# Who issues the stores: gate chunks and the high halves of queries and keys go from ScalarE's queue to SyncE's, and the load of `b_f` goes to the front

## The chip, the cores and the metric

One Trainium2 chip, of which one core is used. The metric is the time of one execution on the device, in microseconds (us). TensorE (PE) multiplies, VectorE (DVE), ScalarE (ACT) and GpSimd (POOL) work on elements, and SyncE (SP) does nothing but issue transfers. Each engine has a queue of its own and works through it in order. A transfer (DMA) is issued by an instruction in one of these queues; the data then move by themselves, and a counter (semaphore) tells when they have landed.

## The reference

One step of a hybrid encoder layer, for a prompt of 1024 rows and a sample of 64 (1088 rows together), in float32. Cut to what matters:

```python
xn = rms_norm(x, g_pre)
xa, ga, q, k, v, gb, fl, ma, mb = split(xn @ w_in)       # widths 7 x 1024 + 16 + ...
logf = log_sigmoid(fl + b_f)
ya = rg_lru(causal_conv(xa)) * silu(ga)                  # branch A, a recurrence over the rows
yb = attention(q, k, v, bias=cumsum(logf)) * silu(gb)    # branch B, 16 heads of 64, causal
u = (ya @ w_branch[0], yb @ w_branch[1])
mix = (sigmoid(ma) * u[0] + sigmoid(mb) * u[1]) @ w_o
h = x + rms_norm(mix, g_post)
y = h + rms_norm(sigmoid(h @ w_ple_gate) * (pe @ w_ple_proj), g_ple)
```

The keys, values, `logf` and the last states are outputs too. The sample attends to a cache of 128 rows as well.

## The kernel before

Every float32 factor is split into a high and a low part, and a product takes three passes on TensorE (high by high, low by high, high by low). ScalarE makes the high part (`copy_act`, L82), VectorE subtracts it from the whole to get the low part (`sub`, L85). So each panel of weights goes through ScalarE and VectorE before TensorE can use it: `w_raw` becomes `wh` and `wl`, and in the opening `wv_raw` becomes `wvh` and `wvl` (the fourth and fifth slices of the value weights are loaded into `w_raw`).

The stages, in order of time:

- **Opening** (to about 125 us). The rows are normalised and turned, and the values (`vacc`, `v_sb`) and the forget logits `fl` are made block by block. `load_wv` (L348) and `load_x` (L338) load on SyncE; `b_f`, which is added to `fl`, is loaded by ScalarE at L505. In the opening the order of ScalarE and VectorE is written out by hand, and each of their instructions stands in the queue where the code says.
- **Plain panels** (to about 162 us). Gate panels: `panel_steps` multiplies a panel of 128 columns by all rows in three chunks, and `spill` (L304) takes each finished chunk out of PSUM into an `st` tile (two buffers) with ScalarE and stores it to memory, to be read again at the end (`d_ma`, `d_mb`, `d_gb` hold the gates of branch A, branch B and the attention's own gate).
- **Quad stage** (about 162 to 430 us). Queries, keys and some gate columns are made by a scheme of seven products for eight (`quad`, L805). `put` (L829) takes a finished half out, and for queries and keys makes a high half `oh` (two buffers) with ScalarE and a low half `kl` or `ko` with VectorE. Both are stored, to be read again by the heads.
- **Attention** (about 437 to 861 us). Sixteen heads, two at a time. Heads load their queries and keys a head ahead. `load_v` (L1069) reads the values of a pair in two halves into `v_raw`, which has one buffer; GpSimd splits them into `vv` (L1077, L85). Scores, softmax (the normalisation is GpSimd's `tensor_scalar`, L1110), transposes (`tp`, split by ScalarE into `th` and by VectorE into `tl`), the product with `vv` (`pv`, L1175 and L1177), and the output `y` (VectorE, L1186) to `d_y` (SyncE, L1162). In between TensorE's time is filled with the chunks of further gate panels, whose `st` is stored by `spill`.
- **Branch A, projections, merge, norms** (from 861 us on). The gates are read back, the recurrence runs, and the last products are made.

TensorE's order is written out by hand from beginning to end. In the attention a planner puts the work of ScalarE, VectorE and GpSimd at booked times (`book`), and the instructions then stand in that order. SyncE's order is the compiler's, except that the four loads of a weight panel keep their order in the program (`load_panel`, L254).

Of the transfers that the change touches, ScalarE issues the stores of `spill`, that of the high half in `put`, and four of the quad stage's gate columns (L838, where the half has no second summand). All other loads and stores are on SyncE already, but for `g8` (L441), the stores of the values (L528) and a few of GpSimd's.

Of the kernel before, what the change touches and what calls it, by code (L numbers as in the profile page):

```python
# [13 lines left out]
P = 128  # L14
# [17 lines left out]
HT = T // 2  # L32
# [33 lines left out]
def hybrid_step(tc, a, o):  # L66
    nc = tc.nc
    PSUM = bass.MemoryType.PSUM
    act, dve, pool, pe, sp = nc.scalar, nc.vector, nc.gpsimd, nc.tensor, nc.sync
# [8 lines left out]
    def f(ap):  # L78
        return ap.bitcast(F32)

    def copy_act(out, in_, scale=1.0):
        return act.activation(out=out, in_=in_, func=AF.Copy, scale=scale)  # L82
# [221 lines left out]
    def spill(dst, t0, n, z, s=None):  # L304
        s = s or wpool.tile([P, GC], F32, name="st")
        copy_act(s[:, :n], z)
        act.dma_start(dst[:, t0:t0 + n], s[:, :n])


    mm = ps("mm", bufs=2)  # L310
# [11 lines left out]
    bf = p1.tile([P, NH], F32, name="bf")  # L322
# [12 lines left out]
    def load_x(b):  # L335
        src, n, _ = x_src[b]
        t = p1x.tile([P, D], F32, name="x_in", tag="x_in", bufs=2)
        sp.dma_start(t[:n, :], src)  # L338
        x_in.append(t)
# [3 lines left out]
    def load_wv(k):  # L343
        if k in (3, 4):
            raw = raw_half[k - 3]
        else:
            raw = p1x.tile([P, D], F32, name="wv_raw", tag="wv_raw", bufs=3)
        sp.dma_start(raw[:, :], w_in[k * P:(k + 1) * P, C_V:C_V + D])  # L348
        raws[k] = raw
# [89 lines left out]
    gT = p1.tile([P, KT], F32, name="gT")  # L439
    load_x(0)  # L440
    act.dma_start(g8[:, :], a["g_pre"].rearrange("(k p) -> k p", p=P))  # L441
    load_wv(0)
    load_x(1)
    for k in range(1, KT):
# [57 lines left out]
    sp.dma_start(g_pre[:, :], a["g_pre"].partition_broadcast(P))  # L502
    load_x(2)
    load_x(3)
    act.dma_start(bf[:, :], a["b_f"].partition_broadcast(P))  # L505
    sp.dma_start(lp[:, :], a["cache_logf"])

    vec = p1.tile([96, P], F32, name="vec")
# [1 line left out]
    for name in ("conv_w", "conv_b", "b_rg_a", "b_rg_x", "a_param", "state_h", "state_conv"):  # L510
        n = a[name].shape[0]
# [70 lines left out]
    for b in range(2, NBLK + 1):  # L582
        _, n, t0 = x_src[b]
# [47 lines left out]
    def gate_panel(tag, w, room=lambda c: None):  # L631
        return panel_steps(mm, *w, xs, lambda c, t0, n, z: spill(tag[1], t0, n, z, room(c)))
# [176 lines left out]
    def keys_out(p, ss, c0, t0, blocks):  # L809

        cols = slice(p * P, (p + 2) * P)
        tp = mm.tile([P, 512], F32, name="tpk", tag="acc")
        c = c0
        for i, n in enumerate(blocks):
            for j, s in enumerate(ss):
                pe.transpose(tp[:n, (2 * i + j) * P:(2 * i + j + 1) * P], s[:, c:c + n], ident[:, :])
            c += n
        for i, n in enumerate(blocks):
            n_st[0] += 1
            st = (wpool.tile([P, GC], F32, name="st") if n_st[0] % 3 else  # L820
                  sp_.tile([P, 2 * P], F32, name="kst", tag="kst", bufs=1))
            copy_act(st[:n, :2 * P], tp[:n, 2 * i * P:2 * (i + 1) * P])
            dst = o["k_prompt"][t0:t0 + n, cols] if t0 < SEQ else o["k_sample"][:, cols]
            sp.dma_start(dst, st[:n, :2 * P])
            t0 += n
# [3 lines left out]
    def put(kind, arg, z, in1, h):  # L829

        s = kqp.tile([P, HT], F32, name="ko", tag="ko", bufs=4)
        s3 = s.rearrange("p (c n) -> p c n", c=2)
        if in1 is None:
            copy_act(s3, z)
        else:
            dve.tensor_tensor(out=s3, in0=z, in1=in1, op=ALU.add)
        if kind == "r":
            (act if in1 is None else sp).dma_start(arg[:, h * HT:(h + 1) * HT], s[:, :])  # L838
            return
        d = d_k if kind == "k" else d_q  # L840
        h_ = slice(h * HT, (h + 1) * HT)
        hi = sp_.tile([P, HT], F32R, name="oh", tag="oh", bufs=2)
        scale = 1.0 if kind == "k" else HD ** -0.5
        copy_act(hi[:, :], s[:, :], scale)
        act.dma_start(d[0, arg][:, h_], f(hi[:, :]))
        lo = sp_.tile([P, HT], F32, name="kl", tag="kl", bufs=1) if kind == "k" else s
        dve.scalar_tensor_tensor(out=lo[:, :], in0=s[:, :], scalar=scale, in1=f(hi[:, :]),
                                 op0=ALU.mult, op1=ALU.subtract)
        sp.dma_start(d[1, arg][:, h_], lo[:, :])
        if kind == "k":  # L850
            kept[arg, h] = s
            p = arg - arg % 2
            if (p, h) in kept and (p + 1, h) in kept:
                ss = [kept.pop((p + j, h)) for j in range(2)]
                c = 0
                for blocks in ((P, P), (P, P), (HT - 4 * P,)) if h == 0 else ((P, P), (P, SEQ - HT - 3 * P), (DEC,)):
                    owed.append((n_prod[0] + 1, lambda c=c, blocks=blocks: keys_out(p, ss, c, h * HT + c, blocks)))
                    c += sum(blocks)

    def seven(i, w, ahead_, last):  # L860
# [28 lines left out]
        if last:  # L889
            mul(tcc, w["s1"], T1, True)  # L890
            for j, t in enumerate(blk(0, 1)):
                sp.dma_start(f(t), d_b12[j])
        mul(ta, w["a12"], B21, False)
        put(*d1, za, None, 0)
        more()
        mul(tb, w["s3"], T3, False)
# [3 lines left out]
        if not last:  # L900
            mul(tcc, w["s1"], T1, True)
        put(*d2, zc, u3, 1)
        mul(tb, w["a22"], T4, False)
        put(*d2, zb, p1, 0)
        more()
        mul(tcc, w["s4"], B22, False)
# [131 lines left out]
    def filler():  # L1038
        left = deque()
        nxt = first_fill  # L1040
        while True:
            if nxt is None:
                look_ahead()
                if not ahead or ahead[0][0][0] != "r":
                    return
                nxt = ahead.popleft()[:3:2]
            (_, dst), w = nxt
            nxt = None
            book_split()

            def evac(c, t0, n, z, dst=dst):
                def do():
                    spill(dst, t0, n, z)
                    left.popleft()

                left.append(book("A", now[0] + 497.0 + HOP_PE, A_ST, do))

            for _ in panel_steps(mm, *w, xs, evac):
                spent(497.0)
                if len(left) > 1:  # L1060
                    catch_up(left[0])
                yield True
# [552 lines left out]
    tag, w = panel()  # L1615
    assert tag == ("f", KT - 1)
    fill = panel_steps(mm, *w, xs, lambda c, t0, n, z: spill(d_mb[KT - 1], t0, n, z))
    chunk(fill)
    early_gate(k - 1)
# [530 lines left out]
    n = x_src[b][1]  # L2150
# [68 lines left out]
```

## Time and profile before

| | us |
|---|---|
| median of three runs | 1465.84 |
| the three runs | 1465.83, 1465.84, 1467.97 |
| the profiled execution | 1464.86 |
| its span in the trace | 1463.1 |
| TensorE busy | 1435.9 |
| VectorE busy | 890.9 |
| ScalarE busy | 717.6 |
| GpSimd busy | 301.8 |

The span goes from the first to the last instruction of the trace; 1.8 us of the execution lie around it. Busy time does not count the instructions that issue transfers. A queue's name with a q (ACTq, SPq) stands for the sequencer that issues: in a row with ACTq, ScalarE is held by an issue. The clock of TensorE has two levels, 1.2 and 2.4 GHz; PEclk gives the granted clock as a share of the higher one.

### The profile page before, as it was taken

To read this page: it belongs to the slowest core of one execution; us is meant where nothing else is said; L and a number is where in the kernel's file an instruction comes from. 1 tells how busy PE (TensorE), PEld (TensorE's weight loads), DVE (VectorE), ACT (ScalarE), POOL (GpSimd) and SP (SyncE) were. 2 spreads that over 40 slices of the span, in tenths; PEclk is the share of its full clock that TensorE was granted. 3 is DMA by queue.
4 is the path that set the end of the run, shared out by engine and by line. 5 is a ranking of instruction groups with operands and counts; after the bars stand their busy time and mean duration, and the time that the engine had idled before them with its cause. 6 is when DMAs were issued, how large, how long until landed. Compare 5 with 4: busy or idle time off the path is not lost.

```text
span 1463.1 us, 25647 instructions
## 1 busy us (share of the span) xinstructions
PE 1435.9 (98%) x9653; PEld 1394.3 (95%) x9653; DVE 890.9 (61%) x1631; ACT 717.6 (49%) x1353; POOL 301.8 (21%) x385
## 2 busy tenths in 40 slices
PE   8999999999999999999899999999999999999997
PEld 8999999999999999999899989999999999879997
DVE  5464866564325666666466555988735474778534
ACT  4423444442215566656466556777534332554633
POOL 0013324323113333333233220221014100000001
PEclk9999999999999999999999999999999999999999
DMA  8457456754276675646554444454269674224111
GB/s 288 141 119 109 139 153 188 182 174 127 81 213 157 119 147 136 142 116 137 109 134 121 76 97 76 90 84 94 75 226 314 242 240 155 97 91 159 51 42 44
DMA packets 149304, 200.64 MB, mean 137 GB/s; under 512 B 24212, under 2 KB 115836, under 8 KB 148156
## 3 DMA queue, kind: packets, MB, share of 16 engines
q1 hardware_dynamic: 129772, 167.06, 44.1%
q10 hardware_dynamic: 17680, 25.64, 5.1%
q0 software_dynamic: 1728, 6.29, 2.3%
q8 instruction: 76, 1.25, 0.4%
q14 instruction: 48, 0.39, 0.1%
HBM read 131.04 MB, written 65.80 MB: 135 GB/s over the span
## 4 chain that ended last, share of the span: by engine, by line
PE 78%; DVE 7%; DMA 6%; ACT 4%; issue 2%; POOL 1%; SPq 1%; ACTq 0%; DVEq 0%; POOLq 0%
PE quad L805 16%; PE acc L170 10%; PE acc L172 10%; PE acc L171 10%; PE tp L1147 4%; PE q L1866 4%; PE pv L1175 3%; PE s L1125 2%; PE pv L1177 2%; PE s L1126 2%; DMA gb_in<-d_gb 2%; PE vacc L170 1%; PE vacc L171 1%; PE vacc L172 1%; POOL yb_in L1671 1%
## 5 line engine op out<-in xcount | busy, mean ns | idle before, releaser
L170 PE MATMUL acc<-xh,wh 128*128 128x364 f32 (+1 forms) x768 | 253.3, 330 | 0.3 <-ACT st L82 0.2
L171 PE MATMUL acc<-xl,wh 128*128 128x364 f32 (+1 forms) x768 | 252.1, 328 | 0.0
L172 PE MATMUL acc<-xh,wl 128*128 128x364 f32 (+1 forms) x768 | 252.0, 328 | 0.0
L170 PEld LDWEIGHTS acc<-xh,wh 128*128 128x128 f32 x768 | 145.0, 189 | 1.7 <-ACT st L82 0.9
L171 PEld LDWEIGHTS acc<-xl,wh 128*128 128x128 f32 x768 | 144.8, 189 | 0.6
L172 PEld LDWEIGHTS acc<-xh,wl 128*128 128x128 f32 x768 | 144.5, 188 | 0.0
L1105 DVE CUSTOM_DVE_ANT_0 s<-s,mask 128x1024 f32<-128x1024 f32 (+7 forms) x128 | 95.5, 767 | 27.7 <-PE s L1126 27.4
L85 DVE TENSOR_TENSOR wl<-w_raw,wh 128x1024 fp32r<-128x1024 f32 (+1 forms) x53 | 60.0, 1134 | 72.1 <-ACT wh L82 71.3
L1110 POOL TENSOR_SCALAR pb<-pb,sm 128x896 f32<-128x896 f32 (+1 forms) x64 | 61.9, 967 | 196.3 <-DVE sm L1109 175.9
L82 ACT ACTIVATE wh<-w_raw 128x1024 fp32r<-128x1024 f32 (+1 forms) x65 | 63.2, 974 | 67.8 <-PE quad L805 26.0
L85 DVE TENSOR_TENSOR tl<-tp,th 128x512 fp32r<-128x512 f32 x96 | 65.8, 688 | 35.8 <-ACT th L82 35.8
L805 PE MATMUL quad<-xh,wh 128*128 128x272 f32 x384 | 80.7, 291 | 0.0
L805 PE MATMUL quad<-xl,wh 128*128 128x272 f32 x384 | 79.5, 288 | 0.0
L805 PE MATMUL quad<-xh,wl 128*128 128x272 f32 x384 | 79.4, 288 | 0.0
L82 ACT ACTIVATE th<-tp 128x512 fp32r<-128x512 f32 x96 | 57.0, 597 | 40.8 <-PE tp L1147 33.3
L1107 ACT ACTIVATE pb<-s,nm 128x896 f32<-128x896 f32 (+1 forms) x64 | 61.1, 955 | 30.1 <-DVE nm L1105 27.7
L1125 PE MATMUL s<-k,q 128*128 128x256 f32 (+1 forms) x192 | 67.4, 354 | 0.2 <-ACT pb L1107 0.2
L1147 PE MATMUL tp<-ident,pb 128*128 128x128 f32 x416 | 64.1, 275 | 1.2 <-DVE diag0l L85 0.7
L1126 PE MATMUL s<-k,q 68*128 68x256 f32 (+1 forms) x192 | 65.2, 351 | 0.0
L171 PE MATMUL acc<-ybl,wh 128*128 128x364 f32 (+1 forms) x192 | 63.0, 328 | 0.9 <-DVE ybl L85 0.9
L170 PE MATMUL acc<-ybh,wh 128*128 128x364 f32 (+1 forms) x192 | 62.8, 327 | 0.2 <-ACT ybh L82 0.2
L172 PE MATMUL acc<-ybh,wl 128*128 128x364 f32 (+1 forms) x192 | 62.8, 327 | 0.0
(713 smaller groups left out, 4154.2 us busy)
## 6 DMA issues: line engine op xcount, KB each, us to landing
w_raw<-in_w_in SPq DMA_DIRECT2D x56, 256.0 KB
q<-d_q SPq DMA_DIRECT2D x48, 256.0 KB
k<-d_k SPq DMA_DIRECT2D x48, 256.0 KB
w_raw<-in_w_in SPq DMA_DIRECT2D x64, 128.0 KB
w_raw<-in_w_branch SPq DMA_DIRECT2D x32, 256.0 KB
wl<-w_raw POOLq DMA_DIRECT2D x12, 512.0 KB, 4.6
wraw<-in_w_in SPq DMA_DIRECT2D x20, 256.0 KB
d_k<-oh ACTq DMA_DIRECT2D x16, 272.0 KB
```

The source lines that it names most:

```text
L82: return act.activation(out=out, in_=in_, func=AF.Copy, scale=scale)
L85: return eng.tensor_tensor(out=out, in0=in0, in1=in1, op=ALU.subtract)
L170: pe.matmul(out, ah, bh, start=start, stop=False)
L171: pe.matmul(out, ah, bl, start=False, stop=False)
L172: pe.matmul(out, al, bh, start=False, stop=stop)
L805: pe.matmul(acc[:, c, :CW], l[:, k, :], r[:, k, c * CW:(c + 1) * CW], start=(first and k == 0 and p == 0), stop=(k == 3 and p == 2), skip_ ...
L1105: at = book("D", now[0] + HOP_PE, per(D_MAX, n), lambda: dve.tensor_tensor_reduce(out=s[:, :n], in0=s[:, :n], in1=m, scale=-1.0, scalar=-N ...
L1107: free = book("A", at, per(A_EXP, n), lambda: act.activation(out=pr[:, :n], in_=s[:, :n], func=AF.Exp, scale=-1.0, bias=nm, accum_out=sm))
L1110: return free, book("G", at, per(G_NORM, n), lambda: pool.tensor_scalar(out=pr[:, :n], in0=pr[:, :n], scalar1=sm, scalar2=1.0, op0=ALU.mul ...
L1125: pe.matmul(s[:, c0:c0 + w], t["q1"][:, q0:q0 + P], t["k1"][:, c0:c0 + w], start=True, stop=False)
L1126: pe.matmul(s[:, c0:c0 + w], t["q2"][:HD + 4, q0:q0 + P], t["k2"][:HD + 4, c0:c0 + w], start=False, stop=True)
L1147: pe.transpose(tp[:, o0 + i * P:o0 + (i + 1) * P], pr[par][:, kb * P:(kb + 1) * P], ident[:, :])
```

## The change

Stores in `spill` and in `put` are issued by SyncE in place of ScalarE, and the load of `b_f` is issued by ScalarE right behind that of `g8`, in place of behind the fourth load of `x`. ScalarE keeps these two loads and the stores of the values.

```diff
     def spill(dst, t0, n, z, s=None):
         s = s or wpool.tile([P, GC], F32, name="st")
         copy_act(s[:, :n], z)
-        act.dma_start(dst[:, t0:t0 + n], s[:, :n])
+        sp.dma_start(dst[:, t0:t0 + n], s[:, :n])
...
     act.dma_start(g8[:, :], a["g_pre"].rearrange("(k p) -> k p", p=P))
+    act.dma_start(bf[:, :], a["b_f"].partition_broadcast(P))
     load_wv(0)
     load_x(1)
...
     load_x(2)
     load_x(3)
-    act.dma_start(bf[:, :], a["b_f"].partition_broadcast(P))
     sp.dma_start(lp[:, :], a["cache_logf"])
...
         if kind == "r":
-            (act if in1 is None else sp).dma_start(arg[:, h * HT:(h + 1) * HT], s[:, :])
+            sp.dma_start(arg[:, h * HT:(h + 1) * HT], s[:, :])
             return
...
         copy_act(hi[:, :], s[:, :], scale)
-        act.dma_start(d[0, arg][:, h_], f(hi[:, :]))
+        sp.dma_start(d[0, arg][:, h_], f(hi[:, :]))
```

## Rows read from the trace of the kernel before

**Rows 1.** The page's first part: busy time of each engine, its share, its instructions.

```profile
PE 1435.9 (98%) x9653; PEld 1394.3 (95%) x9653; DVE 890.9 (61%) x1631; ACT 717.6 (49%) x1353; POOL 301.8 (21%) x385
```

**Rows 2.** TensorE's waits: line, what it waited for, total us, times, longest.

```profile
PE pv L1175 <- DVE y L1186: 4.6, 2, 4.0
PE vacc L471 <- ACT wvh L82: 3.0, 2, 1.9
...
PE quad L805 <- DVE u__1643 L887: 0.9, 1, 0.9
```

**Rows 3.** The table by stretches: length, busy times, PEclk, DMA share, GB/s.

```profile
23.93:31.64 7.71, 7.48 (x37) 7.06 (x38) 6.96 (x13) 5.29 (x8) 0.00 (x0) 0.78 0.95 336
...
714.63:720.72 6.09, 6.09 (x22) 5.91 (x23) 3.73 (x9) 3.37 (x7) 1.38 (x2) 0.50 0.10 24
```

**Rows 4.** Timeline of ScalarE, 18 to 34: start, length, line, idle time before.

```profile
18.85 0.90 ACT L82 ACTIVATE xh<-tp,gT 128x128 fp32r<-128x128 f32 x3
...
22.82 2.00 ACT L82 ACTIVATE wvh<-w_raw 128x1024 fp32r<-128x1024 f32 x2 [3.07 <-DMA vec<-in_conv_b]
...
27.96 1.06 ACT L82 ACTIVATE wvh<-wv_raw 128x1024 fp32r<-128x1024 f32 x1 [1.04 <-DMA wv_raw<-in_w_in]
```

**Rows 5.** The chain of waits, 13 to 45: start, length, what held it.

```profile
14.31 8.06 DMA vec<-in_conv_b
...
22.40 0.38 ACTq L505
...
31.80 5.72 PE vacc L471 x36
```

**Rows 6.** Timeline of ScalarE, 708 to 714.

```profile
708.65 0.46 ACT L82 ACTIVATE st<-acc 128x360 f32<-128x360 f32 x1
...
712.93 0.60 ACT L82 ACTIVATE th<-tp 128x512 fp32r<-128x512 f32 x1 [3.81 <-DMA v_raw<-out_v_prompt]
```

**Rows 7.** The chain of waits, 690 to 716.

```profile
692.15 7.87 DMA d_mb<-st
...
700.50 6.61 DMA v_raw<-out_v_prompt
...
709.56 2.90 DMA v_raw<-out_v_prompt
...
712.53 0.35 ACTq L307
...
714.16 0.42 DVE y L1186
```

**Rows 8.** Timeline of TensorE, 14 to 37.

```profile
21.67 0.32 PE L471 MATMUL acc<-wvl,xh 128*128 128x346 f32 x1
23.93 0.58 PE L471 MATMUL vacc<-wvh,xh 128*128 128x346 f32 x2 [1.94 <-ACT wvh L82]
...
35.93 0.64 PE L471 MATMUL vacc<-wvh,xh 128*128 128x346 f32 x3
```

**Rows 9.** Issues by line: durations in ns (min/median/max), first and last start.

```profile
L307 ACTq DMA_DIRECT2D d_mb<-st x24: 326/326/393, 559.0 to 1029.9; - x24
...
L845 ACTq DMA_DIRECT2D d_k<-oh x16: 326/326/358, 165.4 to 312.1; - x16
```

**Rows 10.** Timeline of TensorE, 709 to 711.

```profile
710.02 0.60 PE L1147 MATMUL tp<-ident,pb 128*128 128x128 f32 x4
```

**Rows 11.** The chain of waits, 128 to 165.

```profile
132.33 0.34 ACTq L307
```

**Rows 12.** Timelines of SyncE and of ScalarE, 748 to 763.

```profile
750.09 6.48 SPq L254 DMA_DIRECT2D w_raw<-in_w_in  x4
...
751.04 0.33 ACTq L307 DMA_DIRECT2D d_gb<-st  x1
```

**Rows 13.** Timelines of GpSimd, 704 to 716 and 758 to 769.

```profile
707.17 0.40 POOL L1077 CAST vv<-v_raw 128x256 fp32r<-128x256 f32 x1 [4.84 <-DMA v_raw<-out_v_prompt]
...
767.88 0.42 POOL L1110 TENSOR_SCALAR prs<-prs,sm 128x192 f32<-128x192 f32 x1 [3.27 <-DVE sm L1109]
```

## The prediction

> **What bounds the kernel now.** I read the page's busy shares first. TensorE is busy for 1435.9 us of the 1463.1 us span [rows 1], so a change of who issues a store can win only where TensorE stands still or runs slowly, some 27 us in all. The list of TensorE's waits comes next: the longest single stops are one of 4.0 us in front of `pv` and one of 1.9 us in front of `vacc` [rows 2]. The table by stretches shows what follows such a stop: from 23.93 to 31.64 the granted clock is 0.78 on average, and from 714.63 to 720.72 it is 0.50, the 1.2 GHz level, with TensorE busy throughout [rows 3]. A stop is thus paid for twice. TensorE's other idle time is in pieces under 1.1 us, the start (1.6 us) and the tail.
>
> Then the chain of waits around both stops, and the timelines of ScalarE and TensorE beside it. Both stops start in ScalarE's queue, at an issue that the change moves.
>
> **First stop: `b_f`.** ScalarE finishes `xh` at 19.75 (18.85 and 0.90) and does nothing until 22.82 [rows 4]. In between its queue holds the issue of `bf`, at 22.40, which the chain puts down to the transfer of `conv_b` that SyncE issued at 14.31 and that needed 8.06 us [rows 5]. `bf` needs nothing of `conv_b`: the two share a completion counter, and the issuing engine waits in order. The split `wvh` stands right behind it. The reader is to see that the idle time in front of `wvh` is put down to that same transfer, not to its own weights: they were there.
>
> **Second stop: `d_mb`.** ScalarE copies `st` at 708.65 for 0.46, so it is free at 709.11, and starts `th` at 712.93 [rows 6]. In between lies the issue of the store of `st`, at 712.53, held by a transfer of `v_raw` that SyncE issued at 709.56 [rows 7]. Up the chain the same pair is tied the other way: a `v_raw` load at 700.50 came late because SyncE had waited for a store of `d_mb` that needed 7.87 us from 692.15.
>
> **The change, part by part.** *The load of `b_f`.* Early in the queue it waits for nothing, and costs ScalarE one issue of 0.38 us [rows 5] before its first work, which waits for `x` in any case; I take nothing for it (at most 0.4 us). The split can then start at 19.75 in place of 22.82. TensorE's last matmul ahead of the stop starts at 21.67, 0.16 after the one before, so the next can start at 21.83 in place of 23.93 [rows 8]. From there to 31.64 it does 36 matmuls; as many at full clock take 5.72 us from 31.80 on [rows 5]. So they would be done at 21.83 + 5.72 = 27.55 in place of 31.64: 4.1 us; with a small new stop, 4.0. If the lower clock stayed, only the stop would go, 1.9 us [rows 2]. What is late next: the last `wv_raw` piece, whose split runs at 27.96 for 1.06 [rows 4]. TensorE takes its slice at 35.93 now [rows 8] and at 31.9 then, so nearly 3 us are left for VectorE's half.
>
> *Stores of gate chunks (L307).* The 24 of `d_mb` take 0.326 us each to issue, the 16 of `d_k` by L845 the same [rows 9]; with 21 of `d_ma`, 12 of `d_gb`, 16 of `d_q` and seven single ones 96 stores leave ScalarE, 31 us of its queue. Nearly all of it is beside the path, as ScalarE has slack. At 709.11, though, it matters: `th` starts then, 3.8 us sooner, and with it `y` at 714.16 - 3.8 = 710.4 for 0.42. TensorE ends its transposes at 710.02 + 0.60 = 710.62 [rows 10], so a stop of about 0.25 is left of 4.00: 3.75 us won. Behind it, 6.09 us were done at half clock [rows 3]; at full clock they take 3.05, as much again. Sum 6.8 us; if the stop stays, nothing.
>
> *Plain panels.* There the chain runs through the issues of L307 themselves, at 132.33 for 0.34 and once more at 152.61 [rows 11], and ends in a stop of 0.9 in front of the first quad product [rows 2]. Taking two issues out gives up to 0.67; the bounds are nothing and 0.9. I take 0.5.
>
> *High halves of query and key, and the four of L838.* They go from ScalarE to SyncE in the quad stage, where the list of waits has one stop over 0.5 us, behind VectorE; I take nothing for them, their cover being TensorE's own matmuls.
>
> **What it adds.** SyncE gets 96 issues more, and it is in order: a store at the head of its queue waits for ScalarE's copy, and each load behind it waits too. One place: SyncE issues four `w_raw` loads from 750.09 on for 6.48 us, while the copy for a store ends at 751.0 and the store leaves ScalarE at 751.04 [rows 12]. Put in front of those loads, it holds them by 0.95 us. What I would fear for is `v_raw`, which has a single buffer and feeds GpSimd. There the trace has one lateness for comparison: GpSimd waited 4.84 us for `v_raw` at 707.17 without a stop of TensorE at that place, and after another pair it stood idle for 3.27 us ahead of 767.88 [rows 13]. Some 3 us of lateness are thus covered by GpSimd's own idle time; behind that its normalisations come late, and TensorE after them. Bounds: nothing, if each delay stays under 3 us, and one stop like that at 714.63 (6.8 us) for each pair of heads that is hit, of which there are seven. As the holds that I can read are nearer 1 us than 3, I take 1 us for small delays.
>
> **The sum.** The profiled execution took 1464.86 us, 0.98 under the median of 1465.84. 1464.86 - 4.0 - 6.8 - 0.5 + 1.0 = 1454.6; beside the median, 1455.5.
>
> **A rule that speaks against it.** The two stops show an issue that cost ScalarE 3.07 and 3.81 us of idle time, ten times its own 0.33. The Trainium skill, "DMA: Bandwidth & Descriptors", section "Issuing engines are not separate DMA queues", says that transfers started by different engines share the same 16 DMA engines, and that spreading the issue saves only the sequencer's time, usually small. By that rule alone the change would be worth the two 0.33 us issues on the chain, and the time about 1465.2. The rows differ from it here, as what ScalarE saves is the wait in front of the issue.
>
> **Rivals.** *One stop comes back.* The wait at 709 is a coincidence of which transfer has the same counter as the store. If SyncE's queue holds `v_raw` or a buffer so that something else is late there, only the start and the panels gain: 1465.84 - 4.0 - 0.5 = 1461.3. For it: the chain there is made of two queues that wait for one another [rows 7], and SyncE is one of them. Against: without the store, nothing in ScalarE's queue waits for SyncE at 709.
>
> *Nothing to be seen.* TensorE stops just as long for another reason behind the same places, or the delays on SyncE give all back: about 1465. By the rule above it is the expected case; the rows above speak against it.
>
> *Slower: the store at the head of SyncE's queue.* SyncE carries the loads of `v_raw`, heads and weights; if its order has stores ahead of them, `v_raw` comes more than 3.3 us late, GpSimd is late with its normalisations, and TensorE stops as it did at 714.63. Against the 11.3 us won, it decides from the third such stop on: 1465.84 - 11.3 + 3 x 6.8 = 1474.9. For it: `v_raw` has one buffer, and SyncE has waited for stores already [rows 7]. Against: 4.84 us of lateness at 707.17 passed without a stop [rows 13].
>
> **How the numbers follow.** A measurement of this kernel tells about 0.2% (2.9 us) from no change. Chances: all three gains, 0.61; one stop back, 0.16; nothing to be seen, 0.13 (with up to two new stops); slower, 0.10. So faster 0.77, same 0.13, slower 0.10. The likeliest is 1455.5, by itself within 1451.5 (0.9 for the panels, no cost on SyncE, some more idle pieces closed) and 1459 (the start at 1.9, or 3 us of delays). The range reaches over the second and third cases, 1451 to 1467, and leaves out the slower one and a little below.
>
> **What the next profile would show.** Right: ScalarE's `wvh` follows `xh` at about 19.8 with no idle time, and the granted clock stays full from there to 40; TensorE's list of waits has no `pv` over 1 us, and the clock is full around 710 as well; the stretch from the quad stage to the tail as long as before. Wrong: a new stop in the head pairs with a half clock behind it, and GpSimd's `vv` waiting for `v_raw` ahead of it; or `w_raw`, queries or keys that come after TensorE wants them. The forecast fails if the order of SyncE's queue is changed so that loads wait for copies by more than 3 us, or if the stops merely move to another store that shares a counter with a late load.

## The result: a little slower, as a new stop takes back what two old ones gave

The changed kernel takes 1468.24 us (median of 22 runs, 1464.60 to 1471.68) where the kernel before takes 1465.84 (22 runs, 1460.98 to 1468.36). The ratio is 1.0024, with an interval of 1.0017 to 1.0032: slower by a quarter of a per cent, and 1.2 us above the range that was forecast. The profiled execution of the changed kernel took 1469.88 us with a span of 1467.9, that is 4.8 us above the span before.

The page of the changed kernel gives TensorE's busy time first (it answers to [rows 1]), and the list of TensorE's waits follows (it answers to [rows 2]; columns as there).

```profile
PE 1433.2 (98%) x9653; PEld 1392.0 (95%) x9653; DVE 894.2 (61%) x1631; ACT 714.6 (49%) x1353; POOL 296.1 (20%) x385
```

```profile
PE acc L170 <- ACT st L82: 12.0, 3, 10.2
...
PE pv L1175 <- DVE y L1186: 1.1, 2, 0.6
PE vacc L472 <- ACT wvh L82: 1.1, 1, 1.1
```

Both old stops are gone: no `pv` waits for more than 0.6 us, where it was 4.0, and the 1.1 us left in front of `vacc` is another stop, ahead of 14 us, which was there before as well. In their place stands one wait of 10.2 us in front of `acc`, for ScalarE's copy `st`. The table by stretches of TensorE (length, busy time, PEclk, DMA share, GB/s; it answers to [rows 3]) shows what this costs.

```profile
22.00:40.00 18.00, 18.00 (x118) 1.00 0.95 307
...
442.09:448.00 5.91, 5.91 (x20) 0.50 1.01 276
707.00:722.00 15.00, 14.35 (x102) 1.00 0.70 111
```

The full clock now holds from 22 to 40 and from 707 to 722. The lower level of 1.2 GHz has moved to the 5.9 us behind the new stop.

The table compares the two traces by the same matmul at each border of a stage: its start in the kernel before is taken from its start in the changed kernel. A minus is time won.

| stretch (by the times before) | us won or lost in it | sum so far |
|---|---|---|
| start to 31.6, the first stop | -4.0 | -4.0 |
| to 161.9, plain panels | +0.5 | -3.5 |
| to 412.5, quad stage | +0.7 | -2.8 |
| to 459.9, start of the attention | +13.0 | +10.2 |
| to 707.9, attention | +0.6 | +10.8 |
| to 720.7, the second stop | -6.7 | +4.1 |
| to the end | +0.6 | +4.8 |

So the two gains came in the size that was forecast, 4.0 and 6.7 us. The loss of 13 us at the start of the attention was not in the sum: 10.2 us are the stop, and 5.9 us at half clock behind it are 2.95 us more than at full clock. The chain of waits of the changed kernel leads to its cause (start, length, what held it).

```profile
424.55 10.76 DMA k<-d_k
435.37 0.27 SPq L1090
...
438.69 0.59 SPq L1097
439.38 2.07 DMA d_ma<-st
441.56 0.48 ACT st L82
```

The timelines of SyncE, ScalarE and TensorE in that stretch show the rest.

```profile
417.22 1.95 SPq L254 DMA_DIRECT2D w_raw<-in_w_in  x4
...
438.20 1.08 SPq L1097 DMA_DIRECT2D qsl<-d_q  x2
439.38 1.00 SPq L307 DMA_DIRECT2D d_ma<-st  x2
...
442.06 0.92 SPq L307 DMA_DIRECT2D d_ma<-st  x2
```

```profile
420.05 0.47 ACT L82 ACTIVATE st<-acc 128x364 f32<-128x364 f32 x1 [6.23 <-PE acc L172]
423.96 0.48 ACT L82 ACTIVATE st<-acc 128x364 f32<-128x364 f32 x1 [3.44 <-PE acc L172]
441.56 1.06 ACT L82 ACTIVATE st<-acc 128x360 f32<-128x360 f32 x2 [17.12 <-DMA d_ma<-st]
```

```profile
442.09 0.67 PE L170 MATMUL acc<-xh,wh 128*128 128x364 f32 x1 [10.16 <-ACT st L82]
```

The first two chunks of the attention stage are copied at 420.05 and 423.96, and both `st` tiles are then full. Their stores leave SyncE only at 439.38, behind 25 loads that begin at 417.22: four of weights, eight for the first head, two of values, eleven for the sample (my expectations below say 26 and twelve). These loads in turn wait for one another in order; the one of `cs_k` at 435.37 was let go by a load of `k` that needed 10.76 us. The instruction records of the traces show why: the transfers of SyncE and ScalarE are dealt out to eight completion counters, SyncE's loads here in turn, so that each stands behind the transfer eight before it; `cs_k` and that load of `k` both have counter 105. In the kernel before, the pairs of the two old stops share a counter in the same way, 109 for `conv_b` and `b_f`, 105 for `v_raw` and the store at 712.53. ScalarE waits 17.12 us for a free `st`, the PSUM banks of `acc` stay full, and TensorE stops for 10.16 us. In the kernel before, ScalarE issued the same two stores at 423.40 and 427.31, between SyncE's loads.

### The profile page after: what moved, and what is told of

Its sections match the earlier page's. It is cut to its first block, busy times and chain, and to the rows that moved or that the text cites. A ratio compares the mean times of both kernels' runs of the same rounds, so it can differ in the third digit from the quotient of the medians.

```text
span 1467.9 us, 25740 instructions
## 1 busy us (share of the span) xinstructions
PE 1433.2 (98%) x9653; PEld 1392.0 (95%) x9653; DVE 894.2 (61%) x1631; ACT 714.6 (49%) x1353; POOL 296.1 (20%) x385
## 4 chain that ended last, share of the span: by engine, by line
PE 79%; DMA 7%; DVE 6%; ACT 4%; issue 2%; SPq 1%; POOL 1%; DVEq 0%; ACTq 0%; POOLq 0%
PE quad L805 16%; PE acc L170 10%; PE acc L171 10%; PE acc L172 10%; PE q L1866 5%; PE tp L1147 4%; PE pv L1175 2%; PE s L1125 2%; PE s L1126 2%; PE pv L1177 2%; DMA gb_in<-d_gb 2%; PE vacc L170 1%; PE vacc L171 1%; PE vacc L172 1%; DMA wl<-w_raw 1%
```

## The experiments

Each was timed against the kernel before on the same chip, where that took 1464.0 to 1464.6 us (the median of each set). Ratios are to it, so versions are compared with one another by their ratios.

**The early load of `b_f` alone.**

```diff
     act.dma_start(g8[:, :], ...)
+    act.dma_start(bf[:, :], a["b_f"].partition_broadcast(P))
...
-    act.dma_start(bf[:, :], a["b_f"].partition_broadcast(P))
```

> The kernel before with one part of the change: the load of b_f right behind that of g8. All stores stay on ScalarE. If the early load alone takes away the first stop: 4.0 us faster than before (about 1461.8 beside 1465.8), the stop of 4.0 us in front of pv near 710 and its half clock stay, and there is no stop at 430 to 450. If the gain in the opening needed the stores on SyncE as well, or is given back in the plain panels: no change, or less than 2 us.

1459.62 us, ratio 0.9970 (0.9959 to 0.9980), by which it is 4.4 us faster. There is no stop near 440, and the old one in front of `pv` stays, as TensorE's list of waits says:

```profile
PE pv L1175 <- DVE y L1186: 4.3, 2, 3.7
```

The first gain is therefore independent of the stores.

**The early load, and only the stores from the 25th on (`d_mb`, `d_gb`) on SyncE.**

```diff
-        act.dma_start(dst[:, t0:t0 + n], s[:, :n])
+        (act if n_sp[0] < 24 else sp).dma_start(dst[:, t0:t0 + n], s[:, :n])
+        n_sp[0] += 1
```

> The kernel before with the early load of b_f and only the stores of gate chunks from the 25th on (d_mb and d_gb) moved to SyncE; those of d_ma, of queries, keys and gate columns stay on ScalarE. Theory: both first forecast gains are independent of the rest, 4.0 + 6.8 us, and nothing stops at 430 to 450: about 1455. Rival, the stop at 710 was removed only by another distribution of counters that came with the other 60 stores: 1461 to 1462.

1455.33 us, ratio 0.9944 (0.9930 to 0.9958). Both gains are there together with the first 24 chunk stores, and those of queries, keys and gate columns, left where they were.

**The changed kernel, with the first four stores of the attention on ScalarE again.**

```diff
-        sp.dma_start(dst[:, t0:t0 + n], s[:, :n])
+        (act if 6 <= n_sp[0] < 10 else sp).dma_start(dst[:, t0:t0 + n], s[:, :n])
+        n_sp[0] += 1
```

> The changed kernel, but the first four stores of gate chunks in the attention stage (d_ma, the ones that the changed kernel issues between 439 and 443) are issued by ScalarE again. My theory now: in the changed kernel these stores stand in SyncE's queue behind 26 loads of weights, heads, values and the sample, so that the two st buffers are not given back, ScalarE waits 17 us for one, and TensorE stops for 10.2 us and then runs 6 us at half clock. By that the stop goes and with it 13.4 us: about 1455 in place of 1468.2. Rival: the loads of the first head are late in any case, because 26 transfers share the engines; then a stop of several us stays between 430 and 445 and the time is above 1462.

1454.79 us, ratio 0.9943 (0.9930 to 0.9955). TensorE no longer stops at 430 to 445, as the table by stretches says (columns as above):

```profile
420.00:450.00 30.00, 29.88 (x184) 1.00 0.84 207
```

Four stores of 96 decide between a gain of 0.6% and a loss of 0.2%.

**The early load, and only those four stores on SyncE.**

```diff
-        act.dma_start(dst[:, t0:t0 + n], s[:, :n])
+        (act if not 6 <= n_sp[0] < 10 else sp).dma_start(dst[:, t0:t0 + n], s[:, :n])
+        n_sp[0] += 1
```

> The kernel before with the early load of b_f and only four of the 96 stores on SyncE: the first four gate chunks of the attention stage. If these four alone make the new stop: 13.4 us slower than with the early load alone (ratio to before near 1.006, about 1473), a stop of 8 to 11 us in front of acc near 441 and half clock behind it; the old stop near 710 stays. If the stop needs SyncE's queue to carry the other 92 stores too: less than 5 us slower than with the early load alone.

1472.12 us, ratio 1.0052 (1.0038 to 1.0065): some 12 us slower than with the early load alone. The list of TensorE's waits, and ScalarE's row where it waits for `st`:

```profile
PE acc L170 <- ACT st L82: 10.1, 1, 10.1
PE pv L1178 <- DVE y L1189: 4.6, 2, 4.0
```

```profile
440.58 0.47 ACT L82 ACTIVATE st<-acc 128x360 f32<-128x360 f32 x1 [17.02 <-DMA d_ma<-st]
```

These four make the new stop by themselves, to a tenth of a microsecond of what the changed kernel shows (10.1 for 10.2). The start of the attention loses 11.8 us here and 13.0 there, as the full clock comes back sooner behind the stop: the granted clock is 0.89 from 444 to 447 here, and 0.50 up to 448 there. The old `pv` stop is back.

**All stores on SyncE, but the 11 loads of the first sample behind the fourth store.**

```diff
     def load_sample(p):
...
+        if p:
+            load_sample_now(p)
...
         sp.dma_start(dst[:, t0:t0 + n], s[:, :n])
+        n_sp[0] += 1
+        if n_sp[0] == 10:
+            load_sample_now(0)
```

> The changed kernel, all its stores on SyncE, but the 12 loads of the first sample (cache, its keys and queries) are issued behind the fourth of those stores in place of in front of the first. Theory of the queue: the first store then leaves SyncE behind the load of pb, some 8 us sooner (at about 431 in place of 439.4), the stop shrinks from 10.2 to 1 to 3 us, and the time is 1456 to 1460. Rival, the store itself or its counter is slow and not its place in the queue: the stop stays over 7 us, and the time within 3 us of 1468.

1462.62 us, ratio 0.9992 (0.9983 to 1.0001), between what the two theories gave. The chain of waits says why.

```profile
420.70 9.35 DMA k<-d_k
...
430.11 6.09 DMA d_ma<-st
...
436.31 0.48 ACT st L82
```

The store left 9.3 us sooner (430.11 for 439.38), as expected, but needed 6.09 us to land in place of 2.07. The stop shrank from 10.2 to 5.7 us. In the changed kernel the first `st` is held for 18.9 us from its copy's end to the issue of its store, and for 2.1 us more until that has landed; here for 10.4 and 6.1. So the place in the queue, still behind 14 loads, is the larger part in both, and the landing is a second one, which my expectation had left out. That it is slow because the loads ahead are still moving fits the DMA engines' busy share, 0.99 from 430 to 437 here and 0.54 from 439.3 to 441.6 in the changed kernel, but no run shows it by itself.

**All 96 stores on SyncE in their places, with room for five chunks in place of two.**

```diff
-        s = s or wpool.tile([P, GC], F32, name="st")
+        if 8 <= n_sp[0] < 11:
+            s = f(p2.tile([P, 512], F32R, name="tl", tag="tl", bufs=3)[:, :])
+        n_sp[0] += 1
+        s = wpool.tile([P, GC], F32, name="st") if s is None else s
```

> The changed kernel with all 96 stores on SyncE in the same order, but the third, fourth and fifth chunk of the attention stage are copied into the three tl buffers of that stage, which are not used before 447, in place of st. Theory: it is the want of a free st buffer that stops ScalarE and then TensorE, not the late landing of the stores; with room for five chunks the stop at 442 goes without any store leaving earlier: 1455 to 1457 in place of 1468.2. Rival, ScalarE or the first head's loads are late for another reason as well: a stop of 3 us or more stays near 435, and the time is over 1460.

1455.64 us, ratio 0.9937 (0.9924 to 0.9950). The first rows are SyncE's and ScalarE's in this kernel, the last one is the table by stretches for TensorE.

```profile
439.56 1.00 SPq L312 DMA_DIRECT2D d_ma<-st  x2
```

```profile
422.96 0.48 ACT L82 ACTIVATE st<-acc 128x364 f32<-128x364 f32 x1 [3.44 <-PE acc L172]
426.96 0.47 ACT L82 ACTIVATE tl<-acc 128x360 f32<-128x360 f32 x1 [3.52 <-PE acc L172]
```

```profile
420.00:450.00 30.00, 29.66 (x183) 1.00 0.87 187
```

The stores leave as late as in the changed kernel (439.56 for 439.38), and TensorE is busy for 29.66 of 30 us. The lateness of these stores costs nothing in itself. What costs is the buffer that each holds.

**The early load, and one store on SyncE: the one that waited at 709.**

```diff
-        act.dma_start(dst[:, t0:t0 + n], s[:, :n])
+        (act if n_sp[0] != 41 else sp).dma_start(dst[:, t0:t0 + n], s[:, :n])
+        n_sp[0] += 1
```

> The kernel before with the early load of b_f and a single store moved to SyncE: the one of d_mb that waited in ScalarE's queue at 709 to 712. All other 95 stay on ScalarE. If this one store is the whole second gain: 6.3 to 6.9 us faster than with the early load alone (ratio to before 0.992 to 0.9935, about 1453 to 1455). If the wait goes over to the next store of ScalarE, or SyncE holds v_raw then: less than 3 us below the early load alone.

1455.06 us, ratio 0.9934 (0.9920 to 0.9948): by the ratios 5.3 us below the early load alone, a little less than expected. By the traces 6.8 us are won between 707.9 and 720.7, and 0.3 in the early load alone, so 6.5. ScalarE's rows show that `th` follows the copy at once, where it stood idle for 3.81 us before [rows 6]:

```profile
704.29 0.46 ACT L82 ACTIVATE st<-acc 128x360 f32<-128x360 f32 x1
704.64 0.60 ACT L82 ACTIVATE th<-tp 128x512 fp32r<-128x512 f32 x1
```

One store brings the whole second gain, and the wait did not go over to another store.

**The stores of queries and keys alone.**

```diff
-            (act if in1 is None else sp).dma_start(arg[:, h * HT:(h + 1) * HT], s[:, :])
+            sp.dma_start(arg[:, h * HT:(h + 1) * HT], s[:, :])
...
-        act.dma_start(d[0, arg][:, h_], f(hi[:, :]))
+        sp.dma_start(d[0, arg][:, h_], f(hi[:, :]))
```

> The kernel before with only the 36 stores of put (high halves of queries and keys, four gate columns) on SyncE; b_f late, all chunk stores on ScalarE. My forecast said nothing for them. Now, from the offset of 0.5 to 0.9 us between 162 and 240 in the changed kernel: 0 to 1 us slower than before, both old stops stay (1.9 at 24, about 4 near 714). If the stop of 4 us near 714 depends on how the counters are dealt out, it changes here too, as 36 stores have gone to another queue.

1464.57 us, ratio 0.9996 (0.9986 to 1.0005): no difference that can be measured. Both old stops stay, though not in their old sizes of 1.9 and 4.0 us:

```profile
PE vacc L471 <- ACT wvh L82: 4.7, 2, 3.6
PE pv L1175 <- DVE y L1186: 4.2, 2, 3.6
```

The first is longer as TensorE came to it 1.9 us sooner, while the split came only 0.25 us sooner. In the trace 0.8 us are lost between 162 and 234, some of it at a stop of 0.5 in front of `tpk` that waits for ScalarE's `st`; the changed kernel loses 0.9 in the same stretch.

**The early load, and the chunk stores from the 11th on.**

```diff
-        act.dma_start(dst[:, t0:t0 + n], s[:, :n])
+        (act if n_sp[0] < 10 else sp).dma_start(dst[:, t0:t0 + n], s[:, :n])
+        n_sp[0] += 1
```

> The kernel before with the early load of b_f and the stores of gate chunks on SyncE from the 11th on; the six of the plain panels, the first four of the attention and all of queries, keys and gate columns stay on ScalarE. By the theory that the 36 stores of queries and keys cost 0.5 us on SyncE (a stop in front of tpk behind the shared queue), that the plain panels gain nothing, and that the stores behind the 10th are free: about 0.5 us below the version with the first four on ScalarE (ratio to before near 0.9935). If the stores of queries and keys are free there: the same as that version.

1456.48 us, ratio 0.9943 (0.9927 to 0.9959). It cannot be told from the other versions near 1455. Its trace loses nothing between 162 and 234, but the 0.5 us do not show in the time.

**The early load, and seven stores: the six of the plain panels and the one at 709.**

```diff
-        act.dma_start(dst[:, t0:t0 + n], s[:, :n])
+        (act if n_sp[0] >= 6 and n_sp[0] != 41 else sp).dma_start(dst[:, t0:t0 + n], s[:, :n])
+        n_sp[0] += 1
```

> The kernel before with the early load of b_f and seven stores on SyncE: the six of the plain panels and the one of d_mb that waited at 709. If the plain panels' stores are worth what the traces suggest (0.6 to 1.3 us of the start's gain are lost at 140 to 162 with them on ScalarE, 0.1 with them on SyncE): up to 1 us below the version with one store moved, that is 1453.5 to 1455 beside 1464.3, and no stop of 0.9 at the first quad product. If they are worth nothing, the stop in front of the quad product stays and the time is the same as with one store.

1454.16 us, ratio 0.9929 (0.9917 to 0.9942), the fastest that was run; its interval overlaps with those of the others near 1455, so it beats both kernels of the study but not them. The stop of 0.9 us in front of the first quad product is gone, but one of 1.6 stands in front of `acc` at 140.4. Between 128 and 162 it loses 0.4 us of the start's gain.

## Why the prediction was wrong

**What bounds the kernel.** Right. What moved the time clear of noise did so through a stop of TensorE and the clock behind it.

**The first stop.** Right, 4.0 us forecast and 4.0 found. ScalarE's rows after, which answer to [rows 4], show that the split follows `xh` at once:

```profile
17.86 1.66 ACT L82 ACTIVATE xh<-tp,gT 128x128 fp32r<-128x128 f32 x6 [0.68 <-DVE xl L435]
19.37 2.04 ACT L82 ACTIVATE wvh<-w_raw 128x1024 fp32r<-128x1024 f32 x2
```

**The second stop.** Right, 6.8 us forecast, 6.7 found, and from 6.7 to 6.9 in the same stretch of the experiments that take it away. A stop of 0.6 us is left of it, where 0.25 was forecast.

**Plain panels.** The gain of 0.5 us is not there: the changed kernel loses 0.5 between 128 and 162. The stop in front of the quad product went, and a longer one came in front of `acc` at 141 (1.66 us for 0.11). There ScalarE's copy stands behind `t4h`, which waits 6.6 us for VectorE's `rc`. With the start 4 us earlier, that chain of VectorE seems to be what comes late next. That is a reading of one trace. The six experiments with these stores on ScalarE lose from -0.1 to 1.0 us there (0.6 on average), the five traces with them on SyncE from -0.3 to 0.5 (0.15 on average). The difference is near the 0.5 that was forecast, but the spread between executions is larger, so it stays open.

**Queries, keys and gate columns.** Nearly right: nothing was forecast, 0.6 to 1.0 us are lost between 162 and 234 in the traces, and no time shows it.

**What it adds.** This step, the cost of the stores on SyncE, failed. It looked at one direction only: loads that stand behind a store and wait for its copy, priced at 1 us. That direction is harmless here. In the changed kernel the loads of `wraw` stand behind three stores of the plain panels and leave 13.9 us later than before (141.74 for 127.85), and no wait of TensorE leads to them; the prediction had named holds of more than 3 us as a sign that it fails. The other direction was not weighed: a store that stands behind loads holds its `st` tile until SyncE has come to it. There are only two such tiles, and 25 loads in a row at the start of the attention take 22 us. The price was 13.0 us in place of 1.0. The other measured terms, -4.0 - 6.7 + 0.5 + 0.7, give -9.5 us. The experiments that only take the four stores out, or give the chunks room, are by their ratios 8.3 and 9.2 us faster than the kernel before, where the forecast was 10.3 (1465.84 to 1455.5). So without this step the forecast would have held within about 2 us.

**The rivals.** "One stop comes back" named a buffer that would be late because of SyncE's queue, but at 709, and priced it as a gain kept back, not as a loss. "Slower" had the right engine and the right in-order queue, with the wrong thing waiting in it: not `v_raw` behind a store, but a store behind the loads of a stage. The rule weighed against it says that spreading the issue saves only the sequencer's time, usually small (the Trainium skill, "DMA: Bandwidth & Descriptors", section "Issuing engines are not separate DMA queues"). These runs do not agree with it in either direction: one store with 0.33 us of issue was worth 5 to 7 us on the other engine, and four of them cost 12 to 13.

## What to carry to other kernels

Before a store is moved to the queue that issues the loads, list for each place what stands ahead of it there, and how long that takes, and hold it against the number of buffers that the stores leave free: the price of a store was here the buffer that it kept, not its issue. A run of loads for a new stage is the place to look first. And where a stall comes from a single issue, move that one: one store and one load gave here what 97 were moved for.

## What the runs showed that was not expected

With the same instructions up to 22 us and the same two stops (1.1 and 0.6 us, at 12.5 and 14.0), the granted clock behind them differs between kernels. The stretch 14.30 to 17.60 of TensorE in the changed kernel, in the one with four stores on SyncE, and in the one with one store moved:

```profile
14.30:17.60 3.30, 3.30 (x17) 0.55 0.53 156
```

```profile
14.30:17.60 3.30, 3.30 (x16) 0.54 0.50 136
```

```profile
14.30:17.60 3.30, 3.30 (x25) 1.00 0.59 164
```

The last gets 25 matmuls into the time of 17, and is 1.3 us ahead afterwards. The kernel before has 0.50 there, and the early load alone 1.00: its trace wins 5.2 us up to 31.6, 1.2 of them up to 17.7, before the place where the load acts. Stops of this size were followed by the lower clock in some of these traces and not in others, so 1 us of difference in one trace of the opening says nothing of a kernel.

Between 1073 and 1143, where the change touches nothing, all traces but one lose 0.4 to 2.8 us against the kernel before (1.1 in the changed kernel), and one wins 0.5. In the changed kernel the chain of waits runs through a late load of `w_branch` there. The cause stays open.
